# The second modulation group of layer 0 computed beside the third, at the end of the attention

## The chip, the cores and the metric

The kernel runs on one core of one Trainium2 chip. The metric is the device time of one execution in microseconds, as the median of several runs. The core has a matrix engine (TensorE, PE in the profile), a vector engine (VectorE, DVE), a scalar engine (ScalarE, ACT), GpSimd (POOL), and SyncE (SP), which in this kernel issues nearly all transfers, in its queue's order. PSUM, into which TensorE writes, has eight banks; here they are split into pools by name. Instructions of one engine run in order; between engines semaphores decide.

## The reference

One inference step of a two-layer backbone with D = 1024 on 128 context and 1024 latent tokens. Layer 0 is what matters here:

```python
mc = jnp.split(sc @ w_mod[i] + b_mod[i], N_MOD, axis=-1)   # context tokens
ml = jnp.split(sl @ w_mod[i] + b_mod[i], N_MOD, axis=-1)   # latent tokens
hl = rmsnorm(xl, norm_mix[i]) * (1 + ml[1]) + ml[0]
ql, kl, vl, pl = even_project(hl, w_in_ab[j], q_gain[j], k_gain[j])
al = neighbourhood_attention(ql, kl, vl, cache_k[:, j], cache_v[:, j], rpb[j])
yl = even_output(al, pl, pool_w[j], pool_scale[j], w_out_ab[j])
xl = xl + ml[2] * yl
hl = rmsnorm(xl, norm_ffn[i]) * (1 + ml[4]) + ml[3]
xl = xl + ml[5] * conv_ffn(hl, ffn_w_in[i], ffn_conv_w[i], ffn_conv_b[i], ffn_w_out[i])
```

The context tokens go the same way with `mc` and an attention over themselves. `sc @ w_mod[i]` is two vectors times a matrix of 1024 x 6144: 24 MB of weights and little arithmetic. Its six parts of 1024 are needed at different times: 0 and 1 before the projections, 2 after the output projection of the mixer, 3 and 4 before the feed-forward part, 5 at the end of the layer.

## The kernel before, in words

All matmuls of the trunk run in float32 as three passes: a weight is split into a high part (`whi`, by ScalarE, L252) and a low part (`wlo`, by GpSimd, L254), the activations into `hhi` and `hlo`.

`mixer0` (L1160) does layer 0's first half. Its stages on TensorE, in the order in which the program is written:

1. `start0`: the norm, and the first modulation group (parts 0 and 1), which arrives in quarters: matmul L506, spread L512.
2. `project_v` (L595): the v projection, 128 tokens x 512 per PSUM bank (`vps`, L610, L611, L613), in two halves, tiles 0 to 5 and then 6 to 8; ScalarE empties the banks (L616).
3. The q and k projections of the first pair of heads (`project_qk`: `qps`, L638, L639, L640, in chunks of 386 or 384 tokens, each in one of two PSUM banks named "aux").
4. The four pooled groups (`project_p`, L454).
5. `attention` (L795): for each of eight heads one unit for the context and four for the latents (k0 to k3). A unit has scores (L701, L702), a softmax on VectorE and ScalarE, transposes of the probabilities (L856, copied by VectorE at L861) and the product with the values (L883, L888). A unit's scores stand next to the previous unit's transposes and products. Twice per unit a `filler` is called: in heads 0 to 5 it takes steps of the next pair's q and k projections, in heads 6 and 7 steps of what stands in the list `mods`.

Then the trunk begins with the output projection (weights `in_woab`).

The modulation of layer 0 comes in three groups of two parts. Groups 1 (parts 2 and 3) and 2 (parts 4 and 5) are made by `mod_group` (L288), a generator of 16 steps. A step loads 512 KB of `w_mod` into a tile `mraw` (SP, L300) and runs two matmuls 32 x 512 with the two conditioning vectors as the stationary operand (L303, both in one PSUM bank `modps`); the profile counts two hardware passes for each, four per step. After 16 steps `mod_spread` (L336) copies the bank to SBUF (L340, VectorE), turns it with four small matmuls (L343, `modt`) and adds the bias (L346, VectorE).

Before, group 1 is the list `early`: `project_v` pulls one step per k of its second half, and `mixer0` pulls one per step of the q and k projections (L1208, L1212). Its tiles are two buffers of the tag "prob" (which the attention uses later for probabilities), its bank is an "aux" one. Group 2 is `mods` (L1228): one step per call of the filler in heads 6 and 7, tiles in turn in the tags `wraw`, `whi` and `wlo` with two buffers each, which the projections no longer need then, and its bank is the only one of the pool "g". What `pull` leaves is flushed behind the attention.

The program's order is not the final one: a scheduler orders the instructions of each engine from the dependences and its own timeline, and the buffers' reuse adds waits.

Of the kernel before, what the change touches and what calls it, by code (L numbers as in the profile page):

```python
# [9 lines left out]
F32 = mybir.dt.float32  # L10
# [9 lines left out]
P = 128  # L20
# [43 lines left out]
def tok0(j):  # L64
    return 0 if j == 0 else L0 + (j - 1) * P
# [60 lines left out]
KP = 0  # L126
LP = 3
PP = 2
RM = 1
RQ = 3  # L130
EK = 0
ER = 1
HN = 6
BANKS = 1, 2, 4, 1
ORDER = "SXfTVg"
# [53 lines left out]
class Kern:  # L189
# [95 lines left out]
        return pss  # L285


    def mod_group(self, l, m, pool, psp, ev, tag="aux", mtag="wraw", last=None):  # L288

        nc = self.nc  # L290
        ps = psp.tile([P, 512], F32, tag=tag, name=self.nm("modps"))
        for k in range(KT):
            for u in range(2):
                if mtag == "prob":
                    raw = pool.tile([P, 2, 640], F32, tag="prob", name=self.nm("mraw"), bufs=2)
                    raw = raw.rearrange("p a b -> p (a b)")[:, :1024]
                else:
                    t = mtag if mtag == "mraw" else ("wraw", "whi", "wlo")[(2 * k + u) // 2 % 3]
                    raw = pool.tile([P, 1024], F32, tag=t, name=self.nm("mraw"), bufs=1 if t == "mraw" else 2)
                nc.sync.dma_start(raw, self.i["wmod"][l, m, k, :, u * 1024:(u + 1) * 1024])  # L300
                for x in range(2):
                    g = 64 * u + 32 * x
                    nc.tensor.matmul(ps[g:g + 32, :], self.sc[:, k, :], raw[:, x * 512:(x + 1) * 512],  # L303
                                     start=k == 0, stop=k == KT - 1)
                yield
        self.mod_spread(l, m, ps, ev, *(last or (psp, tag)))
        yield

    def mod_beside(self, l, m, mp, ev):
# [282 lines left out]
            nc.sync.dma_start(self.cat[4 + g], y[:, :T])  # L592
        return finish

    def project_v(self, hhi, hlo, ready, wv, sp, between):  # L595

        nc = self.nc
        mm = nc.tensor.matmul
        for js in ((0, 1, 2, 3, 4, 5), (6, 7, 8)):
            pss = [self.psm.tile([P, 3, 512], F32, tag="mm3", name=self.nm("vps")) for _ in range(len(js) // 3)]  # L600
            for k in range(KT):
                if js[0] and k >= EK:
                    self.pull(between, ER)
                if k % 2 == 0:
                    whi, wlo = self.wunit(self.i["wv"][k // 2], *((wv.pop(0), nc.vector) if wv else ()))
                    next(ready, None)
                s = slice((k % 2) * 512, (k % 2) * 512 + 512)
                pvs = [(pss[x // 3][:, x % 3, :], tok0(j)) for x, j in enumerate(js)]
                for pv, o in pvs:
                    mm(pv, hhi[k][:, o:o + P], whi[:, s], start=k == 0, stop=False)  # L610
                    mm(pv, hhi[k][:, o:o + P], wlo[:, s], start=False, stop=False)  # L611
                for pv, o in pvs:
                    mm(pv, hlo[k][:, o:o + P], whi[:, s], start=False, stop=k == KT - 1)  # L613
            for x, j in enumerate(js):
                v = sp.tile([P, TS], F32, tag="u", name=self.nm("vst"))[:, :512]
                nc.scalar.activation(v, pss[x // 3][:, x % 3, :], AF.Copy)  # L616
                if j == 0:
                    v3 = v.rearrange("p (h d) -> p h d", h=H)
                    nc.vector.tensor_copy(self.vctx[:, :, 0, :], v3)
                    nc.vector.tensor_tensor(self.vctx[:, :, 1, :], v3, self.vctx[:, :, 0, :].bitcast(F32),  # L620
                                            op=ALU.subtract)
                    nc.sync.dma_start(self.o["nv"], v)
                else:
                    nc.sync.dma_start(self.vd[(j - 1) * P:j * P, :], v)
# [535 lines left out]
    def mixer0(self, dp):  # L1160
        tc, nc, I, cp = self.tc, self.nc, self.i, self.cp
        with ExitStack() as l0:
            pool = lambda n, b, **kw: l0.enter_context(tc.tile_pool(name=n, bufs=b, reuse_waits="tile", **kw))
            vp = pool("vp", 1)
            self.vctx = vp.tile([P, H, 2, DH], F32R, name="vctx")
            self.qm = [vp.tile([P, T], F32R, name=f"qm{b}") for b in range(2)]
            self.km = [vp.tile([P, T], F32R, name=f"km{b}") for b in range(2)]
            up = pool("up", 9)
            ap = pool("ap", 1)
            self.wp = pool("wp", 1, side="right")  # L1170
            self.wbufs = 2
            hp = pool("hp", 16, side="right")
            with ExitStack() as pj:
                self.psm = pj.enter_context(tc.tile_pool(name="psm", bufs=2, space=PSUM, reuse_waits="tile"))
                self.psa = pj.enter_context(tc.tile_pool(name="psa", bufs=2, space=PSUM, reuse_waits="tile"))
                evac = lambda: ap.tile([P, 512], F32, tag="pth", name=self.nm("modev"), bufs=3)
                hhi, hlo, ready, wv = self.start0(up, hp, ap, evac)
                next(ready)
                early = [self.mod_group(0, 1, ap, self.psa, evac, mtag="prob")]
                self.project_v(hhi, hlo, ready, wv, up, early)  # L1180
                for x, ts in enumerate((self.qm, self.km)):
                    raw = up.tile([P, TS], F32, tag="u", name=self.nm("msraw"))
                    nc.sync.dma_start(raw[:, :T], I["masks"][:, x])
                    for b, t in enumerate(ts):
                        oth = slice(64 - 64 * b, 128 - 64 * b)
                        nc.scalar.activation(t[oth, :], raw[oth, :T], AF.Copy)
                raw = self.wp.tile([P, 1024], F32, tag="wraw", name="pwraw", bufs=2)
                nc.sync.dma_start(raw[:, :512], I["pw"])
                self.pwhi = ap.tile([P, 512], F32R, tag="pth", name="pwhi", bufs=3)
                self.pwlo = ap.tile([P, 512], F32R, tag="ptl", name="pwlo", bufs=3)  # L1190
                nc.scalar.activation(self.pwhi, raw[:, :512], AF.Copy)
                nc.gpsimd.tensor_tensor(self.pwlo, raw[:, :512], self.pwhi.bitcast(F32), op=ALU.subtract)
                fin = None
                project, qk = {}, {0: []}
                g0 = self.project_qk(0, 0, hhi, hlo, up, self.psa, "aux", qk[0])
                g1 = self.project_qk(0, 1, hhi, hlo, up, self.psa, "aux", qk[0])

                def filler(h, kind, half):
                    if h < 6:
                        q = project[h // 2 + 1]  # L1200
                        self.pull(q, RQ)
                    else:
                        self.pull(mods, RM)
                att = self.attention(ap, up, qk, project, filler)
                prep = [att]
                for _ in range(7):
                    next(g0, None)
                    self.pull(early, 1)  # L1208
                for _ in range(20):
                    next(g1, None)  # L1210
                    next(g0, None)
                    self.pull(early, 1)  # L1212
                fin = None
                for gg in PF:
                    f = self.project_p(gg, hhi, hlo, up)
                    if fin is not None:
                        fin()
                    fin = f
                    self.pull(prep, PP)
                fin()  # L1220
            with ExitStack() as at:
                ps = lambda n, b: at.enter_context(tc.tile_pool(name=n, bufs=b, space=PSUM, reuse_waits="tile"))
                self.psc, self.pss, self.pst, self.psg = (ps(n, b) for n, b in zip(("psc", "pss", "pst", "psg"), BANKS))
                for pr in range(1, 4):
                    qk[pr] = []
                    project[pr] = [self.project_qk(pr, 0, hhi, hlo, up, self.psg, "g", qk[pr]),
                                   self.project_qk(pr, 1, hhi, hlo, up, self.psg, "g", qk[pr])]
                mods = [self.mod_group(0, 2, self.wp, self.psg, evac, tag="g", last=(self.pst, "w"))]  # L1228

                for _ in att:  # L1230
                    pass
                self.flush(mods)
# [272 lines left out]
```

## Time and profile before

| | |
|---|---|
| median of 3 runs | 2699.41 us (2694.0 to 2701.53) |
| profiled execution | 2696.8 us, its span 2694.8 us |
| mean granted TensorE clock | 0.989 |
| TensorE busy | 2605.4 us (97%) |
| VectorE busy | 1597.6 us (59%) |
| ScalarE busy | 1124.1 us (42%) |
| GpSimd busy | 1244.9 us (46%) |
| DMA | 345.88 MB, mean 128 GB/s |
| group 1's matmuls (L303) | 66.1 to 142.2 us in the span |
| group 2's matmuls (L303) | 445.2 to 484.4 us in the span |

All rows are of the one profiled execution; times in it run from the start of its span. The profiled execution is 2.6 us below the median. A row of the timeline gives the start and duration in us, engine, line, operation, what it computes out of what, the shape, the number of instructions taken together, and in brackets how long the engine sat idle before it and what ended that.

### The profile page before, as it was taken

What the parts mean: (1) busy time and instruction counts of PE and PEld (TensorE: products, weight loads), DVE (VectorE), ACT (ScalarE), POOL (GpSimd) and SP (SyncE); (2) the same over time, 40 slices, a digit from 0 to 9 for tenths busy, and PEclk for the clock granted to TensorE, in tenths of its full rate; (3) what the DMA queues carried; (4) which work ended last, traced back from release to release, by engine and by line L of the source; (5) the groups of instructions that cost most, each with busy time, mean ns of one, the idle gap of its engine ahead of it and who ended that gap; (6) DMA issues with size and microseconds to landing.
All of it is one profiled execution on the core that took longest, in us unless ns stands there. A gap on an engine that the chain in (4) does not pass through costs nothing.

```text
span 2694.8 us, 38615 instructions
## 1 busy us (share of the span) xinstructions
PE 2605.4 (97%) x14982; PEld 2352.9 (87%) x14982; DVE 1597.6 (59%) x2455; ACT 1124.1 (42%) x1743; POOL 1244.9 (46%) x736
## 2 busy tenths in 40 slices
PE   6999998989999999999999999999999999999999
PEld 4698897788999999989998889889999999888887
DVE  6046777493567767654997854379964344444444
ACT  4326666525422222354545364555324323433332
POOL 1322333265433332233556254689757544655553
PEclk9999998999999999999999999999999999999999
DMA  7612235564446555444444553222222222433332
GB/s 283 221 51 79 71 79 142 184 198 135 139 161 205 190 172 179 170 160 141 141 133 133 187 188 102 87 87 76 73 71 71 79 80 70 129 93 95 95 96 89
DMA packets 139734, 345.88 MB, mean 128 GB/s; under 512 B 46112, under 2 KB 51872, under 8 KB 139552
## 3 DMA queue, kind: packets, MB, share of 16 engines
q1 hardware_dynamic: 139552, 343.41, 40.1%
q8 instruction: 119, 1.95, 0.3%
q14 instruction: 63, 0.52, 0.1%
HBM read 291.97 MB, written 46.67 MB: 126 GB/s over the span
## 4 chain that ended last, share of the span: by engine, by line
PE 82%; DVE 10%; ACT 2%; issue 2%; DMA 2%; POOL 1%; SPq 0%; POOLq 0%; DVEq 0%; ACTq 0%
PE mm L264 15%; PE mm L268 15%; PE mm L266 15%; PE mn L264 8%; PE mn L266 8%; PE mn L268 8%; PE mm L454 2%; DVE modacc L324 2%; DVE x L437 2%; PE O L888 2%; DVE dacc L996 1%; PE tp L856 1%; PE qps L638 1%; PE qps L639 1%; PE qps L640 1%
## 5 line engine op out<-in xcount | busy, mean ns | idle before, releaser
L254 POOL TENSOR_TENSOR wlo<-wraw,whi 128x1024 fp32r<-128x1024 f32 x280 | 687.7, 2462 | 909.3 <-ACT whi L252 737.6
L252 ACT ACTIVATE whi<-wraw 128x1024 fp32r<-128x1024 f32 x348 | 364.5, 1057 | 770.8 <-PE mm L266 396.4
L264 PE MATMUL mm<-h,whi 128*128 128x332 f32 (+6 forms) x2208 | 558.3, 323 | 7.1 <-DVE x L437 6.6
L268 PE MATMUL mm<-h,wlo 128*128 128x332 f32 (+6 forms) x2208 | 560.0, 324 | 0.9 <-POOL wlo L254 0.8
L266 PE MATMUL mm<-h,whi 128*128 128x332 f32 (+6 forms) x2208 | 558.6, 324 | 0.0
L264 PEld LDWEIGHTS mm<-h,whi 128*128 128x128 f32 x2208 | 382.6, 189 | 21.5 <-issue 8.6
L268 PEld LDWEIGHTS mm<-h,wlo 128*128 128x128 f32 x2208 | 381.0, 189 | 13.5 <-POOL wlo L254 1.9
L266 PEld LDWEIGHTS mm<-h,whi 128*128 128x128 f32 x2208 | 379.7, 189 | 10.4
L996 DVE SCALAR_TENSOR_TENSOR dacc<-u,params,dacc 128x661 f32<-128x661 f32 (+1 forms) x344 | 285.3, 829 | 7.6
L437 DVE SCALAR_TENSOR_TENSOR x<-mm,mod,x 128x128 f32<-128x128 f32 (+7 forms) x408 | 210.4, 559 | 130.8 <-PE mm L268 129.2
L264 PE MATMUL mn<-h,whi 128*128 128x494 f32 (+1 forms) x672 | 262.5, 391 | 3.2 <-DVE x L437 3.2
L266 PE MATMUL mn<-h,whi 128*128 128x494 f32 (+1 forms) x672 | 262.1, 390 | 0.0
L268 PE MATMUL mn<-h,wlo 128*128 128x494 f32 (+1 forms) x672 | 260.5, 390 | 0.0
L1092 DVE SCALAR_TENSOR_TENSOR facc<-mm,params,facc 128x663 f32<-128x663 f32 (+3 forms) x92 | 82.1, 892 | 275.0 <-ACT facc L1091 274.9
L1092 DVE SCALAR_TENSOR_TENSOR facc<-mn,params,facc 128x493 f32<-128x493 f32 (+1 forms) x84 | 62.0, 738 | 218.6 <-ACT facc L1091 218.5
L264 PE MATMUL mm<-fh,whi 128*128 128x332 f32 (+2 forms) x720 | 171.7, 318 | 14.2 <-DVE x L437 12.3
L268 PE MATMUL mm<-fh,wlo 128*128 128x332 f32 (+2 forms) x720 | 169.5, 315 | 0.0
L266 PE MATMUL mm<-fl,whi 128*128 128x332 f32 (+2 forms) x720 | 169.4, 315 | 0.0
L978 POOL TENSOR_TENSOR acc<-acc,tap 128x508 f32<-128x508 f32 (+1 forms) x104 | 151.3, 1460 | 38.6 <-ACT tap L977 32.6
L1104 POOL TENSOR_TENSOR facc<-facc,facc 128x494 f32<-128x494 f32 (+2 forms) x66 | 91.3, 1383 | 145.1 <-DVE facc L1094 145.1
L437 DVE SCALAR_TENSOR_TENSOR x<-mn,mod,x 128x510 f32<-128x510 f32 (+1 forms) x168 | 120.5, 736 | 63.8 <-PE mn L268 63.0
L1107 ACT ACTIVATE fh<-facc 128x664 fp32r<-128x664 f32 (+3 forms) x88 | 60.2, 684 | 227.5 <-POOL facc L1104 140.1
(227 smaller groups left out, 4539.1 us busy)
## 6 DMA issues: line engine op xcount, KB each, us to landing
wraw<-in_fi_dram SPq DMA_DIRECT2D x176, 512.0 KB
wraw<-in_fo_dram SPq DMA_DIRECT2D x88, 512.0 KB
mraw<-in_wmod_dram SPq DMA_DIRECT2D x48, 512.0 KB
mraw<-in_wmod_dram SPq DMA_DIRECT2D x96, 256.0 KB
wraw<-in_pw_dram SPq DMA_DIRECT2D x48, 512.0 KB
lowi<-wlo SPq DMA_DIRECT2D x44, 512.0 KB
wlo<-lowi SPq DMA_DIRECT2D x44, 512.0 KB
lowo<-wlo SPq DMA_DIRECT2D x22, 512.0 KB
```

Source lines behind the costliest of these rows:

```text
L252: nc.scalar.activation(hi, raw, AF.Copy)
L254: (eng or nc.gpsimd).tensor_tensor(lo, raw, hi.bitcast(F32), op=ALU.subtract)
L264: mm(pv, whi, xhi[:, a:b], start=start, stop=False)
L266: mm(pv, whi, xlo[:, a:b], start=False, stop=False)
L268: mm(pv, wlo, xhi[:, a:b], start=False, stop=stop)
L324: i = nc.vector.scalar_tensor_tensor(acc, rv, c, acc, op0=ALU.mult, op1=ALU.add)
L437: nc.vector.scalar_tensor_tensor(xd[:, a:b], pv, gate[:, d, st:st + 1], xd[:, a:b], op0=ALU.mult, op1=ALU.add)
L978: nc.gpsimd.tensor_tensor(acc[:, :n], acc[:, :n], p[:, :n], op=ALU.add)
L996: nc.vector.scalar_tensor_tensor(acc[:, :n] if t == NCK - 1 else pacc, u[:, t:t + n], wk(i, t), acc[:, :n] if t == side else pacc, op0=ALU ...
L1092: nc.vector.scalar_tensor_tensor(acc[:, 1:W], part.ps(ps, 0, W - 1), w(0), acc[:, 1:W], op0=ALU.mult, op1=ALU.add)
L1104: (nc.gpsimd if side or part.n == 1 else nc.vector).tensor_tensor(a[:, :W], a[:, :W], g[:, :W], op=ALU.mult)
L1107: nc.scalar.activation(hi[:, :W], a[:, :W], AF.Copy)
```

## The change

Group 1 leaves the projections. It is put into the list `mods` ahead of group 2, so both are taken by the filler in heads 6 and 7, each with the tiles in `wraw`, `whi` and `wlo`, the single "g" bank and the spread in the pool `pst`. The filler takes two steps per call instead of one (`RM`). `early`, `EK`, `ER` and the branch with the "prob" tiles go. In the changed program the same lines stand up to 12 lines higher: L303 is L297, L300 is L294, L343 is L337, L638 to L640 are L630 to L632, L701 and L702 are L693 and L694, L789 is L781, L856 is L848, L883 and L888 are L875 and L880.

```diff
-RM = 1
+RM = 2
-EK = 0
-ER = 1
...
-    def mod_group(self, l, m, pool, psp, ev, tag="aux", mtag="wraw", last=None):
+    def mod_group(self, l, m, pool, psp, ev, tag, last):
...
-                if mtag == "prob":
-                    raw = pool.tile([P, 2, 640], F32, tag="prob", name=self.nm("mraw"), bufs=2)
-                    raw = raw.rearrange("p a b -> p (a b)")[:, :1024]
-                else:
-                    t = mtag if mtag == "mraw" else ("wraw", "whi", "wlo")[(2 * k + u) // 2 % 3]
-                    raw = pool.tile([P, 1024], F32, tag=t, name=self.nm("mraw"), bufs=1 if t == "mraw" else 2)
+                t = ("wraw", "whi", "wlo")[(2 * k + u) // 2 % 3]
+                raw = pool.tile([P, 1024], F32, tag=t, name=self.nm("mraw"), bufs=2)
...
-        self.mod_spread(l, m, ps, ev, *(last or (psp, tag)))
+        self.mod_spread(l, m, ps, ev, *last)
...
-    def project_v(self, hhi, hlo, ready, wv, sp, between):
+    def project_v(self, hhi, hlo, ready, wv, sp):
...
-                if js[0] and k >= EK:
-                    self.pull(between, ER)
...
-                early = [self.mod_group(0, 1, ap, self.psa, evac, mtag="prob")]
-                self.project_v(hhi, hlo, ready, wv, up, early)
+                self.project_v(hhi, hlo, ready, wv, up)
...
                 for _ in range(7):
                     next(g0, None)
-                    self.pull(early, 1)
                 for _ in range(20):
                     next(g1, None)
                     next(g0, None)
-                    self.pull(early, 1)
...
-                mods = [self.mod_group(0, 2, self.wp, self.psg, evac, tag="g", last=(self.pst, "w"))]
+                mods = [self.mod_group(0, m, self.wp, self.psg, evac, tag="g", last=(self.pst, "w")) for m in (1, 2)]
```

What the scheduler makes of it is seen in the engines' orders. They differ in the projections and at the end of the attention; the trunk's order is the same.

TensorE at the start of the q projection of the first pair of heads, before. `qps` is a chunk's bank, `modps` the bank of the modulation group, `mraw` a step's tile:

```order
L638 MATMUL qps_774<-hhi_303,whi_768 128x386
L639 MATMUL qps_774<-hlo_304,whi_768 128x386
L303 MATMUL modps_614<-mraw_787,sc 32x512 x2
L640 MATMUL qps_774<-hhi_303,wlo_769 128x386
L638 MATMUL qps_774<-hhi_311,whi_768 128x386
L639 MATMUL qps_774<-hlo_312,whi_768 128x386
L640 MATMUL qps_774<-hhi_311,wlo_769 128x386
```

The same place now:

```order
L630 MATMUL qps_741<-hhi_303,whi_735 128x386
L631 MATMUL qps_741<-hlo_304,whi_735 128x386
L630 MATMUL qps_768<-hhi_303,whi_735 128x384
L631 MATMUL qps_768<-hlo_304,whi_735 128x384
L632 MATMUL qps_741<-hhi_303,wlo_736 128x386
L630 MATMUL qps_741<-hhi_311,whi_735 128x386
L631 MATMUL qps_741<-hlo_312,whi_735 128x386
L632 MATMUL qps_741<-hhi_311,wlo_736 128x386
```

The step of the group between the high and the low weight's passes is gone; in its place stand the first two matmuls of the next chunk (`qps_768`), whose bank is free now.

TensorE around the context unit of head 7, before. `O` is the product with the values (L883 opens a unit's bank), `tp` a transpose, `S` and `C` are scores, `vctx` the context's values:

```order
L883 MATMUL O_4981<-consts,st_4882 64x128
L701 MATMUL C_5001<-ck_4216,qs_4547 128x256
L702 MATMUL C_5001<-ck_4216,qm_156 128x256
L701 MATMUL C_5001<-ck_4216,qs_4547 128x256
L702 MATMUL C_5001<-ck_4216,qm_156 128x256
L856 MATMUL tp_5029<-consts,prob_4958 128x128 x4
L888 MATMUL O_4981<-pth_4977,vctx 128x128
L701 MATMUL S_5090<-ks_4543,qs_4547 128x384
L702 MATMUL S_5090<-km_158,qm_156 128x384
L701 MATMUL S_5093<-ks_4543,qs_4547 128x384
L702 MATMUL S_5093<-km_158,qm_156 128x384
L888 MATMUL O_4981<-ptl_4978,vctx 128x128
```

The same place now, as far as the next unit's opening:

```order
L297 MATMUL modps_4793<-mraw_4955,sc 32x512 x2
L880 MATMUL O_4965<-pth_4961,vctx 128x128
L693 MATMUL S_5086<-ks_4477,qs_4481 128x384
L694 MATMUL S_5086<-km_158,qm_156 128x384
L693 MATMUL S_5089<-ks_4477,qs_4481 128x384
L694 MATMUL S_5089<-km_158,qm_156 128x384
L880 MATMUL O_4965<-ptl_4962,vctx 128x128
L848 MATMUL tp_5030<-consts,prob_4938 128x128 x4
L297 MATMUL modps_4793<-mraw_4973,sc 32x512 x2
L848 MATMUL tp_5039<-consts,prob_4938 128x128 x2
L297 MATMUL modps_4793<-mraw_4977,sc 32x512 x2
L875 MATMUL O_5046<-consts,st_4939 64x128 x2
```

Three steps of group 2 stand where there were none. In all the list has 32 steps from head 6 on, in 23 separate places, where it had 16 in 11; group 1's 16 come first, in 10 places, then its spread, then group 2's in 13 places, and its spread.

SP's queue at the end of the attention, before. `vr` is a piece of the values read for a unit, `cat` the attention's output on its way, `in_woab` the weights of the output projection:

```order
L300 DMA mraw_4935<-in_wmod_dram 128x1024
L789 DMA vr_4939<-vd 128x1x64 x4
L300 DMA mraw_4971<-in_wmod_dram 128x1024
L300 DMA mraw_4989<-in_wmod_dram 128x1024
L300 DMA mraw_5025<-in_wmod_dram 128x1024
L300 DMA mraw_5073<-in_wmod_dram 128x1024
L1289 DMA cat_5367<-cat_66 128x664
L789 DMA vr_4993<-vd 128x1x64 x4
L236 DMA wraw_5435<-in_woab_dram 128x1024
L236 DMA wraw_5441<-in_woab_dram 128x1024
L789 DMA vr_5077<-vd 128x1x64 x4
L236 DMA wraw_5447<-in_woab_dram 128x1024
```

The last part of the same stretch now:

```order
L781 DMA vr_5073<-vd 128x1x64
L294 DMA mraw_4973<-in_wmod_dram 128x1024
L294 DMA mraw_4977<-in_wmod_dram 128x1024
L294 DMA mraw_5013<-in_wmod_dram 128x1024
L781 DMA vr_5162<-vd 128x1x64 x2
L294 DMA mraw_5017<-in_wmod_dram 128x1024
L781 DMA vr_5162<-vd 128x1x64
L294 DMA mraw_5065<-in_wmod_dram 128x1024
L781 DMA vr_5162<-vd 128x1x64
L294 DMA mraw_5069<-in_wmod_dram 128x1024
L294 DMA mraw_5105<-in_wmod_dram 128x1024
L234 DMA wraw_5435<-in_woab_dram 128x1024
```

The loads of the steps now stand between the pieces of the values up to the end, and all the loads of the output projection's weights come behind them.

## The prediction

> **What bounds the kernel now.** I read the page first (span, busy time, slices, chain), then where L303, the group's matmul, stands, then TensorE's timeline at both places, then what each engine waits for there.
>
> ```profile
> span 2694.8 us, 38615 instructions
> PE 2605.4 (97%) x14982; PEld 2352.9 (87%) x14982; DVE 1597.6 (59%) x2455; ACT 1124.1 (42%) x1743; POOL 1244.9 (46%) x736
> PE   6999998989999999999999999999999999999999
> PE 82%; DVE 10%; ACT 2%; issue 2%; DMA 2%; POOL 1%; SPq 0%; POOLq 0%; DVEq 0%; ACTq 0%
> ```
>
> TensorE is busy for 97% of the span and carries 82% of the chain that ended last. Whatever stands in its instruction stream counts nearly in full, except where it idles anyway. So two questions decide: what TensorE pays for a group in the projections, and what it will pay for the same group at the attention's end. The next rows are windows cut down to L303: the first window holds the group in the projections, the second the other group at the attention's end. The columns are us, busy TensorE with the number of hardware passes, weight loads, granted clock, share of DMA time, GB/s.
>
> ```profile
> 66.00:150.00 84.00, 16.06 (x64) 2.09 (x64) 0.96 0.57 185
> 440.00:486.00 46.00, 13.30 (x64) 2.12 (x64) 0.93 0.72 206
> ```
>
> The same 64 passes take 16.06 us in one place and 13.30 in the other. They come in 14 runs in the projections and in 11 at the attention's end, a run being steps with no other matmul between them. TensorE's timeline shows what a run costs (start, duration, line, what it computes, number of passes, idle time before it and its releaser):
>
> ```profile
> 72.80 1.06 PE L303 MATMUL modps<-mraw,sc 128*32 128x512 f32 x6
> 82.38 1.06 PE L303 MATMUL modps<-mraw,sc 128*32 128x512 f32 x8
> 83.41 0.50 PE L610 MATMUL vps<-whi,hhi 128*128 128x512 f32 x1
> 107.66 1.05 PE L303 MATMUL modps<-mraw,sc 128*32 128x512 f32 x4 [1.72 <-DMA mraw<-in_wmod_dram]
> 108.64 0.45 PE L640 MATMUL qps<-hhi,wlo 128*128 128x386 f32 x1
> 112.73 1.05 PE L303 MATMUL modps<-mraw,sc 128*32 128x512 f32 x4
> 115.33 0.44 PE L638 MATMUL qps<-hhi,whi 128*128 128x384 f32 x1 [1.54 <-ACT qsq L644]
> 130.93 1.49 PE L303 MATMUL modps<-mraw,sc 128*32 128x512 f32 x4 [1.45 <-DMA mraw<-in_wmod_dram]
> 445.15 2.78 PE L303 MATMUL modps<-mraw,sc 128*32 128x512 f32 x24 [0.61 <-DVE qk L660]
> 465.60 1.05 PE L303 MATMUL modps<-mraw,sc 128*32 128x512 f32 x4
> ```
>
> Four passes (one step) take 1.05 us and eight take 1.06: up to two steps, a run has one price. Six steps together take 2.78. A rule of the Trainium skill fits: "TensorEngine Tiling (Array Packing)", section Tiling Modes, says that a change of the tiling mode drains TensorE. The shapes agree (128*32 beside 128*128, where the others have 128*128), and so does the equal price of 4 and 8 passes. The rule speaks against this change, and comes back as a rival.
>
> **Taken out of the projections.** The order has no step and no spread of this group there any more: 14 runs and one spread go.
>
> ```profile
> PE vps L613 <- DVE hlo L529: 3.6, 1, 3.6
> PE modps L303 <- DMA mraw<-in_wmod_dram: 3.6, 3, 1.7
> PE qps L638 <- ACT qsq L644: 1.5, 1, 1.5
> 147.94 1.06 PE L343 MATMUL modt<-consts,modev 128*128 128x8 f32 x8
> 81.78 3.05 ACT L616 ACTIVATE vst<-vps 128x512 f32<-128x512 f32 x6 [7.76 <-PE vps L613]
> 134.70:202.00 67.30, 67.30 (x422) 62.34 (x422) 27.04 (x40) 14.76 (x25) 14.18 (x18) 1.00 0.19 50
> ```
>
> The first three rows are all that TensorE waits for there (total, times, longest). The sum, in us:
> - The runs' busy time, 16.06, less the run at 82.38 (1.06): the vps matmul behind it needs a bank that ACT's copies empty from 81.78 on, so it waits with or without the run. Leaves 15.0.
> - The three waits of L303 for its own tiles go with it: 3.6.
> - The wait of L638 for the copies of the first 386-column chunk: 1.5. Now both "aux" banks are free, and the order puts matmuls of chunk 1 there instead.
> - The spread's four transposing matmuls: 1.06. Its copy and two additions on VectorE are hidden in the full row 134.70:202.00, where TensorE never idles and VectorE is busy for 27 of 67 us.
>
> That is 21.2. What is late next takes some of it back:
>
> ```profile
> 97.15 2.40 POOL L254 TENSOR_TENSOR wlo<-wraw,whi 128x1024 fp32r<-128x1024 f32 x1 [5.70 <-ACT whi L252]
> 103.36 1.06 ACT L252 ACTIVATE whi<-wraw 128x1024 fp32r<-128x1024 f32 x1 [3.60 <-DMA wraw<-in_wab_dram]
> 104.49 2.37 POOL L254 TENSOR_TENSOR wlo<-wraw,whi 128x1024 fp32r<-128x1024 f32 x1 [3.37 <-ACT whi L252]
> SPq L300 <- PE modps L303: 25.3, 9, 12.5
> ```
>
> The low half of the first q weight is ready at 104.49 + 2.37 = 106.86, and its first reader L640 starts at 108.64 before. With about 7 us less ahead of it TensorE would be there near 101.6. The weight can come sooner as well: SP stood 25.3 us behind L303 for free "prob" tiles, with the weight loads behind it in its queue, and that stops. I take a wait of 1.5 there, 0.9 for the last quarter of the first group (its spread now stands six to eight vps matmuls later, and the 3.6 us wait for hlo hangs on it) and 0.8 for the v weight at 97.15: together 3.2, so a gain of **18.0**. Its bounds: 21.2 if nothing is late, and about 12 if the q weight comes no sooner at all (then what was saved ahead of 107.66 is lost in front of L640, and what remains from there on is 1.72 + 1.05, 1.05 + 1.54, 1.45 + 1.49, four more runs of 1.06 and the spread's 1.06, together 13.6, less about 1.6 for the weights behind). The DMA issues that leave SP's queue cost nothing elsewhere. That the group's results are ready later matters only at the end of the mixer, where the first output projection's gate reads them.
>
> **Added at the attention's end.** The order shows the two groups one after the other: 10 runs and a spread, then 13 runs and a spread, against 11 runs and one spread. So 12 runs more at 1.05 and a spread more at 1.01:
>
> ```profile
> 501.44 1.01 PE L343 MATMUL modt<-consts,modev 128*128 128x8 f32 x8
> 500.36 0.69 DVE L340 COPY modev<-modps 128x512 f32<-128x512 f32 x1
> 469.75:477.55 7.80, 7.80 (x47) 4.58 (x46) 4.39 (x15) 4.65 (x17) 0.73 (x1) 1.00 0.82 241
> 477.55:485.55 8.00, 8.00 (x48) 4.46 (x46) 3.85 (x14) 4.87 (x17) 0.00 (x0) 1.00 0.70 242
> 485.55:492.52 6.97, 5.40 (x37) 4.26 (x37) 4.56 (x15) 6.00 (x14) 5.67 (x4) 1.00 0.11 21
> 492.52:498.15 5.63, 5.53 (x39) 4.66 (x39) 5.21 (x19) 5.34 (x15) 4.21 (x4) 1.00 0.68 196
> 498.15:506.34 8.19, 6.37 (x46) 5.61 (x47) 7.01 (x26) 6.53 (x23) 1.45 (x2) 1.00 0.26 76
> PE O L888 <- DVE ptl L861: 3.0, 2, 2.1
> PE O L883 <- DVE ptl L861: 2.7, 3, 1.6
> ```
>
> 12 x 1.05 + 1.01 = 13.6. The windows (us, then TensorE, weight load, VectorE, ACT, POOL, clock, DMA share, GB/s) go from one unit of the attention to the next. Where the group runs today TensorE is full (7.80 of 7.80, 8.00 of 8.00). Behind it TensorE idles 1.57 + 0.10 + 1.82 = 3.5 us, waiting for VectorE's ptl. Nine of the 12 added runs and the added spread come behind 492.52 and one or two more in 485.55:492.52, so at best 3.5 of the 13.6 goes into this idle time: 10.1. VectorE gets one copy and two additions more, and has room (4.56 to 7.01 busy per row). Both groups use the one "g" bank, so the second's first step waits for the copy of the first (0.69); I cost that at nothing, because some twenty rows of attention matmuls stand between in the order; without them it would be the 0.69.
>
> The queues: SP gets 16 more loads here. Six buffers (three tags of two) let a load go out six steps ahead of its use, and 32 steps from 445.15 to 506.34 and 11 us more are one each 2.3 us; five such are 11 us of lead.
>
> ```profile
> 450.55 0.30 PE L701 MATMUL C<-ks,qs 128*128 128x128 f32 x1 [1.52 <-DMA ks<-ks]
> 530.00:540.00 10.00, 10.00 (x68) 10.00 (x67) 1.39 (x4) 1.65 (x2) 1.71 (x2) 1.00 1.02 409
> SPq L300 <- PE modps L303: 1.4, 2, 1.2
> ```
>
> 16 loads of 512 KB are 8.4 MB, 20.5 us at the 409 GB/s that this core reaches at full share. Free in the five windows are 18% of 7.80, 30% of 8.00, 89% of 6.97, 32% of 5.63 and 74% of 8.19, that is 17.9 us, and the stage itself gets some 11 longer: enough. Two of the loads now stand ahead of the ks copies on SP, for which TensorE waits 1.52 us already, and the five loads of the output projection's weights now follow the last step, so ACT's and POOL's splits of them come late: between nothing and 5 for both (two 512 KB loads at 241 GB/s are 4.4 us), and I take 0.9, since most loads are issued well ahead of their use. So the attention grows by **11.0**, between 8 (the drain behind the last unit covers more than the idle time shown) and 19 (13.6 and the 5).
>
> **Sum.** -18.0 + 11.0 = -7.0. The profiled execution took 2696.8 us around its span of 2694.8, which gives 2689.8; from the median of the runs, 2699.4, it gives 2692.4. I put it between, at **2691**. What a measurement of this kernel tells from no change is about 0.3%, 8.1 us, so the forecast lies at that edge: a gain, which may or may not be seen.
>
> **Rivals.**
> - *The drain alone counts.* By the Tiling Modes rule the price follows the changes of mode: 13 paying runs go at 1.06 and 12 come at 1.05, a gain of 1 us, and the spreads cancel. This holds if the waits that left the projections (3.6 and 1.5) reappear as waits for weights, and the 3.5 idle at the attention's end, set by VectorE's chain, moves along with the runs instead of swallowing them. For it: the equal price of 4 and 8 passes. Against it: 25.3 us of SP's waiting ends, so the weights should come sooner. It gives some 2695 to 2700, within 0.3%.
> - *More is hidden.* The projections give the full 21.2 and the attention takes 8: -13, 2684 to 2686. For it: the attention's last part idles, and DMA was at share 0.57 throughout the projections' window. Against it: TensorE is full from 469 to 485.
> - *Slower: loads too late at the attention's end.* If the stage doesn't stretch to give DMA its room, 20.5 us of loads meet 17.9 free, and every late tile holds TensorE in order, with vr and the output weights behind it on SP. It decides once a load takes longer than the 11 us of lead. Price: 19 there, against only 12 gained: +7, 2704 to 2706. The trace shows what else a wait brings:
>
> ```profile
> 60.00:70.00 10.00, 7.84 (x22) 5.29 (x23) 7.85 (x12) 2.17 (x4) 1.02 (x1) 0.66 0.26 78
> ```
>
> Around the 3.6 us wait for hlo the granted clock is 0.66. The Trainium skill, "TensorE: Matmul & The Clock Gate", Part 1, has the clock halved after an idle window of about 3.4 us; the row agrees, and one such stall at the attention's end would come with slower matmuls behind it. Against this rival: SP's waits for L303 there are 1.4 us in all today.
>
> **Chances and range.** A gain of 4 to 11 as summed: 0.58, a bit over half of it beyond 8.1 us. Drain alone or otherwise within 4 us of before: 0.20. More hidden: 0.13. Slower: 0.09, some of it within 0.3%. So faster 0.46, same 0.46, slower 0.08. The range, 2682 to 2701, holds the likeliest case from both starting points, the larger gain, and no change; it leaves out the slower case and the far end of the larger gain.
>
> **What would show it.** In the projections L303 is gone, the wait of L638 for qsq too, and the q projections' last matmul of head pair 0 comes 15 to 21 us sooner; a wait for wlo ahead of L640 or for hlo above 4 us would show my 3.2 too small. At the attention's end 23 runs of the step, each about 1.05, and from the first ks matmul of head 6 to the end 8 to 14 us more. A step waiting for its load there, or a granted clock under 1 in the 40 us ahead of the end, would show the slower rival. The trunk behind keeps its order, so any difference there beyond 1 us would be a term that I don't have.

## The result and the profile after

The changed kernel takes 2684.3 us (median of 4 runs, 2682.85 to 2686.94) against 2699.49 before: ratio 0.9947, interval 0.9933 to 0.9961. In a second series it took 2684.62 (5 runs), ratio 0.9944 (0.9931 to 0.9956). It is 15 us faster by the medians and 0.53% by the ratio, and neither interval holds "no change". The profiled execution took 2686.94 us, the longest of the four, and before's 2696.8 lies 2.7 us under its median; so the two profiles are only 9.9 us apart, and a later profile of the same changed kernel had a span of 2678.3.

The page of the changed kernel:

```profile
span 2685.2 us, 38619 instructions
PE 2600.6 (97%) x14982; PEld 2352.7 (88%) x14982; DVE 1590.9 (59%) x2455; ACT 1123.3 (42%) x1743; POOL 1244.6 (46%) x736
PE 81%; DVE 11%; ACT 3%; issue 2%; POOL 1%; DMA 1%; SPq 0%; POOLq 0%; DVEq 0%; ACTq 0%
```

TensorE is as full as before, on a shorter span. Where the time went is seen by stages. I read in TensorE's timelines when the attention's first score matmul starts, when the output projection's first matmul starts, and when the trunk's last matmul on `h` does (its very last one, on `fh`, comes 11.1 us later in all three):

| us | projections (to the first score) | attention (to the output projection) | trunk (to its last matmul on `h`) |
|---|---|---|---|
| before | 225.1 | 292.4 | 2160.5 |
| after | 202.3 | 303.3 | 2163.0 |
| after, second profile | 199.6 | 301.9 | 2160.4 |

The projections gave 22.9 us (25.6 in the second profile), the attention took 10.9 (9.5), and the trunk differs by 2.5 in one profile and by nothing in the other. Together that is 9.4 us less in the first profile and 16.1 in the second; the medians' 15 lies between.

TensorE's waits from 28 to 226 us, after (total, times, longest), and L297, which is L303 of before:

```profile
PE pw L582 <- ACT pdh L573: 2.2, 1, 2.2
PE qps L630 <- ACT whi L250: 2.2, 1, 2.2
PE C L693 <- ACT py L585: 1.5, 1, 1.5
PE qps L632 <- POOL wlo L252: 1.5, 1, 1.5
PE vps L602 <- ACT hhi L522: 1.2, 2, 0.8
PE vps L602 <- ACT vst L608: 1.0, 1, 1.0
...
L297 PE MATMUL modps<-mraw,sc x128: 592/593/759, 419.1 to 491.0; 128*32 128x512 f32 x128
```

The 3.6 us wait for hlo and the 3.6 us for the group's loads are gone. New are 2.2 and 1.5 for the high and low half of the first q weight, and 1.0 for the bank that ACT empties (which the run at 82.38 hid before). The 32 steps of the two groups start between 419.1 and 491.0.

At the attention's end there is a wait that before didn't have: two steps wait for their loads. The total, the two steps, and the 10 us behind them:

```profile
PE modps L297 <- DMA mraw<-in_wmod_dram: 3.8, 2, 2.5
424.90 1.05 PE L297 MATMUL modps<-mraw,sc 128*32 128x512 f32 x4 [1.31 <-DMA mraw<-in_wmod_dram]
428.40 1.22 PE L297 MATMUL modps<-mraw,sc 128*32 128x512 f32 x4 [2.45 <-DMA mraw<-in_wmod_dram]
429.00:439.00 10.00, 9.79 (x47) 7.76 (x43) 6.30 (x17) 2.51 (x8) 0.74 (x1) 0.66 0.99 279
```

The first six steps run together at 419.08 and take all six tiles, SP issues the loads of the seventh and eighth from 420.44 on, and TensorE is there from 423.6 on, some 3 us later. Behind the waits the granted clock is 0.66. In the second profile these waits are 2.9 us.

Why the wait for hlo went is seen on VectorE. Rows of before, then of after, around the chain that makes hlo from the third quarter of the first modulation group (x, then hlo):

```profile
51.29 5.15 DVE L525 SCALAR_TENSOR_TENSOR x<-rs,g,x 128x130 f32<-128x130 f32 x4
56.36 0.83 DVE L529 SCALAR_TENSOR_TENSOR hlo<-x,md,hhi 128x130 fp32r<-128x130 f32 x1
57.22 1.60 DVE L773 CAST ck<-craw 64x256 fp32r<-64x256 f32 x2
58.85 3.52 DVE L529 SCALAR_TENSOR_TENSOR hlo<-x,md,hhi 128x1024 fp32r<-128x1024 f32 x2
```

```profile
49.99 1.71 DVE L765 CAST ck<-craw 64x256 fp32r<-64x256 f32 x2 [2.93 <-DMA craw<-in_ck_dram]
52.42 3.57 DVE L519 SCALAR_TENSOR_TENSOR x<-rs,g,x 128x130 f32<-128x130 f32 x4
55.91 3.97 DVE L523 SCALAR_TENSOR_TENSOR hlo<-x,md,hhi 128x130 fp32r<-128x130 f32 x3
```

Before, two casts of the cached keys stand inside the chain (57.22 to 58.85) and x takes 5.15; after, they stand ahead of it, in time that VectorE waited anyway, and x takes 3.57. From the start of x to the end of hlo it is 11.1 us before and 7.5 after: of these 3.6 us the casts are 1.6, and x is another 1.6. While x is slow GpSimd's L254 runs beside it (52.90, 2.45 us); after, that one ran ahead of x (48.42), since its weight had landed sooner. That this is what slows x is not shown. The casts wait for the keys' load, which on SP comes behind group 1's second load before and behind none after.

### The profile page after: what moved, and what is told of

The parts are those of the page before. It is cut to its first block, busy times and chain, and to the rows that moved or that the text cites. A ratio compares the mean times of both kernels' runs of the same rounds, so it can differ in the third digit from the quotient of the medians.

```text
span 2685.2 us, 38619 instructions
## 1 busy us (share of the span) xinstructions
PE 2600.6 (97%) x14982; PEld 2352.7 (88%) x14982; DVE 1590.9 (59%) x2455; ACT 1123.3 (42%) x1743; POOL 1244.6 (46%) x736
## 4 chain that ended last, share of the span: by engine, by line
PE 81%; DVE 11%; ACT 3%; issue 2%; POOL 1%; DMA 1%; SPq 0%; POOLq 0%; DVEq 0%; ACTq 0%
PE mm L262 15%; PE mm L264 15%; PE mm L266 15%; PE mn L262 7%; PE mn L264 7%; PE mn L266 7%; DVE dacc L988 2%; PE mm L448 2%; DVE modacc L318 2%; DVE x L431 2%; PE O L880 2%; PE qps L630 1%; PE qps L632 1%; PE tp L848 1%; PE qps L631 1%
```

## The experiments

Each was timed beside the kernel before on the same chip (its median there 2698.4 to 2699.0). Line numbers in their profiles may differ by a few.

**What the group costs at the attention's end.** `third_only` is the changed kernel without group 1:

```diff
-    mods = [self.mod_group(0, m, ...) for m in (1, 2)]
+    mods = [self.mod_group(0, m, ...) for m in (2,)]
+    self.mod_bias(0, 1)      # the results are the bias alone
```

> The changed kernel without group 1: its loads, steps and spread are left out, and its results are the bias alone. Theory (the attention pays what the forecast summed, 11 us, and the projections gave 22.9): against the changed kernel the projections stay as they are, to 1 us, and the attention's last two heads get 10 to 12 us shorter, so about 2673. Rival (the mode change alone, nothing hidden in idle time): 13.6 us shorter, 2670.5. Rival (the group is mostly hidden there): under 6 us shorter, above 2678.

Measured: 2671.97 us, ratio 0.9903 (0.9888 to 0.9918). The first score came at 203.8, the attention took 294.3: 9.0 less than in the first profile of the changed kernel, 7.6 less than in its second. By the ratios the whole is 12 us shorter than the changed kernel, but each ratio's interval is 4 us to either side, so the stage is the better measure. TensorE's longest waits from 436 us on, first of this kernel, then of the changed one:

```profile
PE O L880 <- DVE ptl L858: 2.7, 3, 1.9
PE O L880 <- DVE st L721: 2.1, 1, 2.1
PE O L885 <- DVE ptl L858: 1.0, 1, 1.0
```

```profile
PE O L875 <- DVE ptl L853: 1.3, 2, 0.8
PE O L880 <- DVE ptl L853: 0.8, 1, 0.8
PE O L875 <- DVE st L726: 0.7, 1, 0.7
```

And the runs there, from the windows cut down to the step's line, `third_only` and then after:

```profile
418.00:500.00 82.00, 14.17 (x64) 2.16 (x64) 0.92 0.49 137
```

```profile
418.00:494.00 76.00, 28.02 (x128) 4.25 (x128) 0.96 0.79 238
```

13.9 us of runs are added and cost 8 to 9: TensorE's waits from 436 us on, the shorter ones included, shrink from 7.2 to 3.6, and the clock granted in these windows is 0.96 instead of 0.92. So the group costs a little less than the 10 to 12 of the theory, and neither the 13.6 of the drain alone nor the under 6 of a group that is mostly hidden. It isn't all of the 10.9, either: `third_only` has 16 steps at the attention's end, as before has, and its attention is still 1.9 us longer than before's (one profile of each). It takes two steps per call, and its seventh and eighth step wait 3.6 us for their loads, as those of the changed kernel do; in before no step there waits for its load.

**What two loads do in the projections.** `two_loads` is the changed kernel with group 1's first two loads put back, and nothing that reads them:

```diff
+    for u in range(2):
+        raw = ap.tile([P, 2, 640], F32, tag="prob", ...)
+        nc.sync.dma_start(raw..., I["wmod"][0, 1, 0, :, u * 1024:(u + 1) * 1024])
     self.project_v(hhi, hlo, ready, wv, up)
```

> The changed kernel plus group 1's first two 512 KB loads where the kernel before had them on SP's queue; nothing reads them. Theory: these two loads push back the loads of the cached keys behind them, so that VectorE's casts of the keys stand inside the chain that makes hlo, and TensorE waits for hlo again for 3 to 4 us, with a granted clock under 0.8 behind it: 4 to 6 us slower than the changed kernel, at the end of the v projection already. Rival (the wait went because group 1's steps and their mode changes left TensorE's order): no wait for hlo above 1 us, the time of the changed kernel within 1.5 us.

Measured: 2687.0 us, ratio 0.9962 (0.995 to 0.9975), over the changed kernel by 2.7 us in the medians and 4 in the ratios. Its waits, two windows (60 to 66 and 66 to 76 us) and VectorE's chain:

```profile
PE vps L605 <- DVE hlo L523: 3.2, 1, 3.2
...
60.00:66.00 6.00, 2.77 (x9) 1.96 (x8) 5.92 (x7) 0.73 (x1) 2.41 (x2) 0.75 0.28 68
66.00:76.00 10.00, 10.00 (x34) 8.18 (x34) 6.50 (x11) 4.01 (x5) 0.00 (x0) 0.64 0.10 40
...
59.36 0.83 DVE L523 SCALAR_TENSOR_TENSOR hlo<-x,md,hhi 128x130 fp32r<-128x130 f32 x1
60.22 2.64 DVE L765 CAST ck<-craw 64x256 fp32r<-64x256 f32 x2
62.90 1.55 DVE L523 SCALAR_TENSOR_TENSOR hlo<-x,md,hhi 128x1024 fp32r<-128x1024 f32 x2
```

With two loads alone, and none of the group's matmuls, the casts are back inside the chain, x is slow again (6.06 us from 53.37 on), TensorE waits 3.2 us for hlo, and the granted clock is 0.75 from 60 to 66 and 0.64 in the 10 us after. The v projection ended 8.9 us later than after (101.3 against 92.4), the first score 5.7 later (208.0). The rival, by which the group's place in TensorE's order made the wait, is out. Over all the kernels here it is the same: the five with these two loads in the projections wait 2.4 to 3.6 us for hlo, the seven without them have no such row among their waits. In those seven the first score came between 199.6 and 204.3, so the two loads cost 3.7 to 8.4 us there; 5.7 is the figure against the first profile. By the attention's end 2.4 us of it are left in this profile.

**Leaving the v projection alone.** `second_after_v` is the kernel before with one number changed:

```diff
-EK = 0
+EK = 8
```

> The kernel before, with group 1's steps pulled only after the v projection (EK 8 instead of 0), among the q and k projections; the loads of the first two steps stay where they were. Theory: the v projection gives 13.3 of the 22.9, of which 4 to 6 hang on the two loads and stay lost; so the v projection ends 7 to 9 us sooner than before, the eight steps or so that move pay 1.05 each later, and the whole is within 2 us of the kernel before or a little slower, since the steps then also wait for their loads. Rival (the cost in the v projection is the steps' place among matmuls that would be better undisturbed): 5 us or more faster than before.

Measured: 2698.79 us, ratio 1.0001 (0.9992 to 1.001). The whole is as the theory had it, its parts were not: the v projection ended 4.1 us sooner, not 7 to 9, and the first score came 4.4 us later than before, not level. The wait for hlo stayed with the two loads:

```profile
PE vps L613 <- DVE hlo L529: 2.9, 1, 2.9
```

The steps cost more among the q projections and the pooled groups than in the v projection.

**Matmuls without their loads.** `one_tile` is the kernel before with 14 of group 1's loads left out; every step multiplies by the first two tiles:

```diff
+    if k == 0:
+        raw = pool.tile(...); held[u] = raw...
+        nc.sync.dma_start(...)
+    raw = held[u]
```

> The kernel before with 14 of group 1's 16 loads left out: every step multiplies by the first two tiles, so group 1's results are wrong and its matmuls, spread and first two loads stay. The scheduler then puts the steps in five runs (1, 3, 4, 11 and 1 steps). Theory: the loads' waits (3.6), the wait behind them (1.5) and the half clock around them go, and the runs shrink from some 15 to 11 us, while the wait for hlo, which hangs on the first two loads, stays at 3 to 4: the first score of the attention comes 8 to 11 us sooner than before, the whole 2688 to 2692. Rival (the loads are nearly all of the price and TensorE's matmuls are hidden): 15 us or more sooner. Rival (the matmuls are nearly all): under 5 us sooner.

Measured: 2693.21 us, ratio 0.9979 (0.997 to 0.9988). The first score came at 215.5, 9.6 us sooner than before, inside the 8 to 11; of this 5.5 were lost in the attention (297.9 against 292.4), for which I have no cause, so the total missed the 2688 to 2692. The wait for hlo stayed, as it should:

```profile
PE vps L617 <- DVE hlo L533: 3.0, 1, 3.0
```

(The five runs hold the group's 16 steps; the counts in the expectation add up to 20.)

Together: of the 22.9 us that the projections gave in the first profile, 5.7 are what the first two loads do to the chain of hlo, 9.6 go with the other 14 loads and the runs that they break up, and the 7.5 left are for the matmuls in few runs and the spread; this last part is the difference and was not measured by itself. Each part is a difference of two single profiles, good to some us only, and `one_tile` changes the loads and the number of runs at once.

**What a run costs.** The price of a run was put down to the drain of a mode change in the prediction. Rows of the changed kernel speak for something else: one run of three steps, and a single one.

```profile
469.65 1.91 PE L297 MATMUL modps<-mraw,sc 128*32 128x512 f32 x12
472.98 1.05 PE L297 MATMUL modps<-mraw,sc 128*32 128x512 f32 x4
```

With the rows before (4 passes 1.05, 8 passes 1.06, 24 passes 2.78) a run costs 0.86 for each up to two steps, and some 0.2. Each single pass in these runs starts 0.43 us after the one ahead in its own group of 32 columns, and the passes of different groups start within 0.02 us of each other: the four groups work side by side, and one step used two of them. `narrow_after` uses all four in each step:

```diff
-    for x in range(2):
-        g = 64 * u + 32 * x
-        matmul(ps[g:g + 32, :], self.sc[:, k, :], raw[:, x * 512:(x + 1) * 512], ...)
+    for x in range(4):
+        matmul(ps[32 * x:32 * x + 32, 256 * u:256 * u + 256], self.sc[:, k, :],
+               raw[:, x * 256:(x + 1) * 256], ...)
```

> The changed kernel with each step's 1024 columns as four matmuls of 32x256, one for each group of 32 columns of the array, instead of two of 32x512 in two of the groups. The work is the same. Theory (the four column groups run side by side, and a run costs two passes of 0.43 us for each up to two steps plus some 0.2): a single step costs 0.6 to 0.7 instead of 1.07, and with some 20 runs the attention's end gets 6 to 9 us shorter: 2675 to 2679. Rival (the price is the drain of the mode change): a step still costs 1.0 or more, and the time is that of the changed kernel within 2 us.

Measured: 2678.82 us, ratio 0.993 (0.9918 to 0.9943). Two of its runs, and all of them in one window:

```profile
461.29 1.50 PE L296 MATMUL modps<-mraw,sc 128*32 128x256 f32 x24
464.81 0.64 PE L296 MATMUL modps<-mraw,sc 128*32 128x256 f32 x8
410.00:494.00 84.00, 20.01 (x256) 6.11 (x256) 0.94 0.73 229
```

A step costs 0.64 instead of 1.05, all runs 20.0 us instead of 28.0, and the attention (295.0) is 8.3 us shorter than in the first profile of the changed kernel, 6.9 than in its second. The drain is at most the 0.2 that is left per run. Once more:

> The changed kernel with the four 32x256 matmuls once more, to see whether it beats the changed kernel beyond the intervals. Theory: 2676 to 2681, the attention's end 6 us or more shorter than the changed kernel's. Rival: within 2 us of the changed kernel's 2684.5.

Measured: 2677.87 us, ratio 0.9924 (0.9911 to 0.9937), attention 296.4. In both series it lies 5 to 7 us under the changed kernel by the medians, 4 to 6 by the ratios. The intervals overlap by a rim (0.9918 to 0.9943 and 0.9911 to 0.9937 against 0.9933 to 0.9961 and 0.9931 to 0.9956), so the ratios alone don't settle it; the stage, 5.5 to 8.3 us shorter in each pair of profiles, shows where the time went. It is the fastest version here that does all the work, 20 us under before.

The same narrow step in the kernel before, `narrow_before` (the same edit):

> The kernel before with each step as four matmuls of 32x256 in the four column groups. Theory: a single step costs 0.68 instead of 1.07 in the projections as at the attention's end; 13 runs there and 10 of one step behind give some 5 and 4 us, 9 in all, less what turns into waits for the steps' loads (the three waits of 3.6 grow): 2691 to 2695. The wait for hlo stays. Rival (in the projections the loads set the pace, not the runs): nothing before the first score, only the 4 us at the end.

Measured: 2687.07 us, ratio 0.9963 (0.9951 to 0.9976), below the range I gave. The first score came only 1.9 us sooner (223.2), which is no more than two profiles of one kernel differ by: in the projections the rival's time holds. Its reason is not shown: the waits for the group's own loads didn't grow but fell from 3.6 to 0.9, and a wait of 2.3 for the first q weight is new, which before didn't have. At the attention's end, with 16 steps, it gave 6.9 (285.5 against 292.4) where I had 4.

**The slower rival, made to happen.** `narrow_three` is the narrow version with three steps per call, `one_step` the changed kernel with one:

```diff
-RM = 2
+RM = 3      # narrow_three;   RM = 1 in one_step
```

> The changed kernel with the four 32x256 matmuls and three steps per call. Theory: the steps stand earlier and in fewer runs (the last one ahead of the last units), but are limited by the loads' bandwidth: the attention's end comes within 2 us of the version with two steps, 2677 to 2681. Rival (fewer runs count): 3 us or more faster than that.

Measured: 2692.62 us, ratio 0.9978 (0.9965 to 0.999), so 14 us slower than with two steps; both of my cases missed. A wait, two steps and a window:

```profile
PE modps L296 <- DMA mraw<-in_wmod_dram: 8.4, 7, 2.2
480.60 1.08 PE L296 MATMUL modps<-mraw,sc 128*32 128x256 f32 x8 [2.16 <-DMA mraw<-in_wmod_dram]
483.16 1.08 PE L296 MATMUL modps<-mraw,sc 128*32 128x256 f32 x8 [1.48 <-DMA mraw<-in_wmod_dram]
470.00:490.00 20.00, 12.60 (x102) 5.79 (x100) 4.76 (x15) 5.23 (x14) 1.91 (x3) 0.74 0.82 275
```

Here the loads come too late: 8.4 us of waits in seven places, the same matmul then takes 1.08 instead of 0.64, at a granted clock of 0.74. This is the rival of the prediction by its mechanism, one step per call away, and nearly by its price: the attention took 309.2, 16.8 more than before, where the prediction had 19. The changed kernel has the same wait in small, 3.8 us.

> The changed kernel with one step per call of the filler instead of two, so that group 1 takes heads 6 and 7 alone and group 2's 16 steps all stand behind the last unit's scores. Theory (lead and bandwidth of the loads decide there): 16 loads of 512 KB take 20 us at 409 GB/s and the stretch behind the last scores has some 15, so TensorE waits for loads there, 5 to 10 us in all, with a granted clock under 1: 2688 to 2694. Rival (the idle time of the last units takes the steps in): within 2 us of the changed kernel or faster.

Measured: 2688.81 us, ratio 0.9968 (0.9956 to 0.998), as the theory's total. Its mechanism was another: no step waited for its load. The output projection's first matmul did, for its weights, whose loads stand behind the last step's on SP:

```profile
PE mm L262 <- ACT whi L250: 4.6, 1, 4.6
```

**The control.**

> The changed kernel once more, as the control on this chip. Theory: the stages up to the trunk repeat to 1 us (first score of the attention at 202.3, trunk from 505.6), since they are set by fixed waits; in the trunk, whose order is that of the kernel before, its length against the kernel before differs from execution to execution by up to 3 us in steps at VectorE waits where the granted clock falls. Rival: the 2.5 us longer trunk of the first profile belongs to the changed kernel; then it shows again at the same place, 820 to 880 us.

Measured: 2684.62 us. The stages didn't repeat to 1 us: the first score came at 199.6 instead of 202.3. Nor did the trunk's 2.5 us. TensorE's wait for the high half of the q weight was 0.9 us in the second profile, where it was 2.2 in the first; the 1.5 for the low half is in both. The window 92 to 104 us of the first profile and of the second:

```profile
92.00:104.00 12.00, 8.30 (x36) 7.50 (x35) 0.00 (x0) 8.90 (x11) 4.74 (x2) 0.86 0.87 288
```

```profile
92.00:104.00 12.00, 9.63 (x52) 8.79 (x52) 0.00 (x0) 8.88 (x11) 4.76 (x2) 1.00 0.85 289
```

With the longer wait the clock is 0.86, with the shorter one 1.00. In the trunk, the window 865 to 880 of before, of after, and of the second profile:

```profile
865.00:880.00 15.00, 14.97 (x99) 14.73 (x98) 10.88 (x19) 2.61 (x3) 2.40 (x1) 1.00 0.53 172
```

```profile
865.00:880.00 15.00, 12.94 (x76) 12.69 (x75) 15.00 (x20) 2.12 (x2) 6.03 (x2) 0.89 0.42 128
```

```profile
865.00:880.00 15.00, 14.39 (x85) 14.42 (x86) 11.06 (x14) 3.98 (x4) 8.43 (x3) 0.89 0.56 178
```

The second profile has the 0.89 there too, with TensorE busier, and its trunk is as short as before's; so the row shows where the first profile lost time, and not that the changed kernel must. Over all kernels here the trunk took 2158.9 to 2163.4 us, though the edits end ahead of it, and the first score of like projections came within 4.7 us. A stage's difference of less than some 5 us between two single profiles is therefore no finding by itself.

## Why the prediction was right, and where not

- **Direction and range.** A gain, inside 2682 to 2701. The size was off: 7 to 8 forecast, 15 measured. Among the cases named the time lies in "more is hidden" (2684 to 2686), but not by its mechanism: the projections gave more than its 21.2, which was also the forecast's own upper bound, and the attention took not 8 but 9.5 to 10.9. That the range still held is owed to its width.
- **"A gain of 18.0" in the projections is the term that was mis-sized: 22.9 and 25.6.** The step of it that failed is "0.9 for the last quarter of the first group", booked against the gain because the spread stands later "and the 3.6 us wait for hlo hangs on it". It doesn't: that wait ends at 62.15 with the hlo of the third quarter, and the last quarter's spread (L512) starts behind it, at 64.50. The wait that I thought would grow went away. I had read in its row that it waits for VectorE's hlo and not asked what VectorE did ahead of hlo, or what SP's queue held ahead of that. `two_loads` shows it: 5.7 us hang on two loads that I called costless ("The DMA issues that leave SP's queue cost nothing elsewhere"). With 5.7 for the gain instead of 0.9 against it, and 2.2 more for the q weight (below), 18.0 becomes 22.4.
- **The clock.** Waits of 1.5 to 3.6 us were followed by a lower granted clock in some places and not in others: 0.66 in the row of 60 to 70, 0.81 around the wait of 1.45 at 130.93, 1.00 from 107.66 to 112.00, behind the wait of 1.72. I showed the 0.66 row, but used it for the slower rival alone. The wait at 130.93:

```profile
126.00:135.00 9.00, 7.52 (x41) 5.94 (x38) 0.18 (x1) 1.38 (x4) 6.45 (x6) 0.81 0.72 211
```

- **"A wait of 1.5 there".** The q weight's halves cost 2.2 + 1.5 in the first profile and 0.9 + 1.5 in the second, more than I took, and the bank for the run at 82.38 the 1.0 that I had said stays.
- **"The attention grows by 11.0"** held as a number: 10.9 and 9.5. Its parts did not, so the closeness is in part luck. The runs besides the spread were 13.9, against my 12.6. More was swallowed than my 3.5 of idle time: with the spread 14.9 were added, and they cost 8 to 9. The 0.9 for the output projection's weights didn't come; its first matmul at 505.59 waits for nothing. And the loads, which I had keep up, didn't quite: 3.8 us of waits (2.9 in the second profile), with a clock of 0.66 behind them. My lead of 11 us took the steps to come evenly, and the first six come as one run. `narrow_three` shows what more of this costs.
- **"The equal price of 4 and 8 passes" as the drain.** This reading was wrong, and the rival built on it with it. The rule of the Trainium skill ("TensorEngine Tiling (Array Packing)", Tiling Modes) may hold, but here it can account for at most 0.2 us of a run's 1.05; the rest is 0.86 for two passes, which 8 passes in four groups take as well as 4 in two. What the same page of the Trainium skill says of the tiles (Key Properties: they work independently) is what the rows show.

## What to carry to other kernels

A load that nobody waits for can still cost: follow what stands behind it in its queue, and what the work that this feeds stands ahead of on an engine that runs in order. When work that needs large loads is moved, give it few enough steps per stretch that each load is there in time; one step per call too many turned the best version here into one that is 14 us slower. A run that uses up all the buffers at once leaves the steps right behind it without a lead. When a matmul uses only some of the array's column groups, split it so that all of them work, before asking where to hide it.

## What the runs showed of the hardware

Four matmuls with 32 stationary columns each, in different column groups, ran side by side: two passes of 512 columns took 0.86 us whether two or four groups were in use (runs of 1.05 and 1.06), and at 256 columns a whole step took 0.64.

A pass of 512 columns in these runs comes 0.43 us after the last one of its group, where the trunk's passes with 128 stationary columns and 512 moving ones came every 0.23 us. The 32 columns are not the reason. `sc` and `mraw` are plain float32, the trunk's operands are fp32r, and the plain float32 passes of L749 with 128 stationary columns are 0.43 apart as well: two passes of 0.59 us each in 1.02 us.

```profile
336.54 1.02 PE L749 MATMUL rev<-tr,consts 128*128 128x512 f32 x2
```

And a wait of about 2 us may or may not be followed by a lower granted clock. Ahead of `pw`, a matmul of the pooled groups, TensorE waits 2.2 us for ScalarE's `pdh` in the changed kernel and in `narrow_after` alike. The 10 us from the end of that wait, first in the one, then in the other (0.67 and 1.00):

```profile
197.20:207.20 10.00, 8.41 (x28) 7.36 (x29) 6.08 (x7) 8.56 (x14) 2.75 (x2) 0.67 0.60 182
```

```profile
195.90:205.90 10.00, 7.88 (x43) 7.06 (x43) 6.92 (x7) 9.07 (x16) 2.78 (x2) 1.00 0.71 205
```
